# Feed-forward products by seven half-size products in place of eight (Strassen), in a two-layer trunk on one core

## The chip, the core and the metric

One core of one Trainium2 chip runs the whole program in one launch. The metric is the time of the execution on the device in microseconds (us), lower is better. The engines are named as the profile names them: PE (TensorE, the matmuls), PEld (its weight loads), DVE (VectorE), ACT (ScalarE), POOL (GpSimd), SP (SyncE, which issues the loads).

## The reference, cut to what matters

A trunk of two layers over 512 tokens of width 1024, all in float32. Each layer is a mixer (attention of two kinds) and then a feed-forward of inner width 2816; the change is about the feed-forward.

```python
D_MODEL, SEQ, DEPTH = 1024, 512, 2
D_FF = 2816
def swiglu(h, w1, w3, w2):
    return (jax.nn.silu(h @ w1) * (h @ w3)) @ w2
...
        x = x + even_mixer(...) if layer % 2 == 0 else x + odd_mixer(...)
        h = rms_norm(x, norm_ffn_g[layer])
        x = x + swiglu(h, ffn_w1[layer], ffn_w3[layer], ffn_w2[layer])
```

## The kernel before

Tokens stand along the free side (512 columns), features on the 128 partitions. The residual stream is eight tiles `xs[c]` of 128x512. To get float32 accuracy out of PE's one-pass float32r matmuls, each operand is split into a high and a low part, and each product is three matmuls: high by high, high by low, low by high (`prods`, L204 to L206).

A weight piece is a block of 128 output features by 1024 inputs (128x1024 in SBUF). SP loads it into one of three `raw` buffers, ACT copies it to the high part (`wh`, L176), DVE subtracts to get the low part (`wl`, L187); the parts rotate through three pairs of buffers (`wsp`).

`ffn` goes through 22 pieces `f` of the inner width. For each it makes the two projections (w1 and w3, eight k-blocks by three matmuls of 128x512 each) into two PSUM banks; then DVE multiplies by the norm's factor `rb` (L308), ACT takes Silu, POOL multiplies by `rb` (L311), DVE multiplies the two projections (L312), ACT and DVE split the product into `gh` and `gl` (L318). Then, for eight output blocks `n`, the down projection w2 sums over 22 blocks, and DVE adds the result to `xs[n]`. `Norm` makes the split input of the next stage (ACT `hh` L253, DVE `hl` L254, and a sum of squares on POOL, L265).

Each engine runs its own queue in order. The order in the queues is made by a scheduler from the order of the code; the orders of the two mixers (`EVEN_ORDER`, `ODD_ORDER`) are tables written out by hand, and the change leaves both as they are.

Of the kernel before, what the change touches and what calls it, by code (L numbers as in the profile page):

```python
# [8 lines left out]
F32 = mybir.dt.float32  # L9
# [7 lines left out]
P = 128  # L17
# [7 lines left out]
# which engines split the weights of a part in two, where not (act, dve)  # L25
# [25 lines left out]
# the order in which the parts are put to the scheduler  # L51
# [65 lines left out]
def tile_trunk(ctx, tc, x, gains, qk_gain, pool_scale, w_a, w_nat, pool_w, w_o0, w_qk, w_v, w_o1, w13, w2, out):  # L117
# [5 lines left out]
    wraw = ctx.enter_context(tc.tile_pool(name="wraw", bufs=WRAW))  # L123
    wsp = ctx.enter_context(tc.tile_pool(name="wsp", bufs=3))
# [4 lines left out]
    # PSUM banks by hand, the one given back first is taken first  # L129
# [78 lines left out]
    class Bank:  # L208
        """A PSUM bank that several sums share: its first product opens it, the others follow that one."""
# [22 lines left out]
    def half(ps, w, acts, i):  # L232
        """The first or the second half of a sum over eight."""
        prods(ps, [(wcol(w, k), acts[k]) for k in range(4 * i, 4 * i + 4)], i == 0, i == 1)

    class Norm:
        """Holds x * gain split in two parts, and the sum of squares."""

        def __init__(self, idx):
            self.idx = idx  # L240
            self.h = [None] * KC
            self.acc = None

# [4 lines left out]
        def scaled(self, c):  # L248
            xt = xs[c]
            g = gain_t[:, self.idx, c : c + 1]  # L250
            hi = res.tile([P, T], F32R, name=f"hh{self.idx}_{c}", tag=f"hh{c}")
            lo = res.tile([P, T], F32R, name=f"hl{self.idx}_{c}", tag=f"hl{c}")
# [40 lines left out]
    def ffn(layer, nrm, nxt):  # L293
        with tc.tile_pool(name=f"ffn{layer}", bufs=1) as fp:
            gs = []
            for f in range(NF):
                wa = weights(w13[layer, f, 0], f"ffn_w1_{layer}_{f}")
                wb = weights(w13[layer, f, 1], f"ffn_w3_{layer}_{f}")
                p1 = take()
                dense(p1, wa, nrm.h)  # L300
                if f == 0:
                    nrm.stats()
                p3 = take()
                dense(p3, wb, nrm.h)
                if f == 0:
                    nrm.bcast()
                a = fp.tile([P, T], F32, name=f"a_{layer}_{f}", tag="fa", bufs=2)
                ve.tensor_mul(a, p1, nrm.rb)  # L308
                s = fp.tile([P, T], F32, name=f"s_{layer}_{f}", tag="fs", bufs=2)
                ac.activation(s, a, AF.Silu)  # L310
                gp.tensor_mul(s, s, nrm.rb)  # L311
                ve.tensor_mul(a, p3, s)  # L312
                give(p1)
                give(p3)
                gh = fp.tile([P, T], F32R, name=f"gh_{layer}_{f}")
                gl = fp.tile([P, T], F32R, name=f"gl_{layer}_{f}")
                ac.copy(gh, a)
                ve.tensor_sub(gl, a, f32(gh))  # L318
                gs.append((gh, gl))
            for n in range(KC):  # L320
                ps = take((n,))
                pairs = []
                for k0 in range(0, NF, 8):
                    k1 = min(k0 + 8, NF)
                    raw = wraw.tile([P, D], F32, name=f"raw_w2_{layer}_{n}_{k0}", tag="raw")
                    cols = (k1 - k0) * P
                    nc.sync.dma_start(raw[:, :cols], w2[layer, n, :, k0 * P : k1 * P])
                    w = split(raw, f"ffn_w2_{layer}_{n}_{k0}", cols)
                    pairs += [(wcol(w, k - k0), gs[k]) for k in range(k0, k1)]
                prods(ps, pairs)  # L330
                ve.tensor_add(xs[n], xs[n], ps)  # L331
                give(ps)
                if nxt is not None:
                    nxt.chunk(n)
                else:
                    nc.sync.dma_start(out[n * P : (n + 1) * P, :], xs[n])

    def even(nrm, nxt, w_first):
        with ExitStack() as es:
            ap = es.enter_context(tc.tile_pool(name="ev", bufs=1))  # L340
            wk = es.enter_context(tc.tile_pool(name="evw", bufs=2))
            OWN = [slice(0, 64), slice(64, 128)]

            one = ap.tile([P, 1], F32, name="one")
# [7 lines left out]
            # low parts of the keys, zero on the half that is not the group's  # L352
# [3 lines left out]
            # v by group, zero on the other group's columns  # L356
# [12 lines left out]
            def both(dst, src, j):  # L369
                """Both parts of a head's half of src, the low one on the other half of the partitions."""  # L370
# [6 lines left out]
            # index queries, raw; a positive factor of a row leaves its order alone  # L377
# [10 lines left out]
            # index keys, on both halves, and the index weights  # L388
# [37 lines left out]
            # index scores; the first block keeps every causal key  # L426
# [21 lines left out]
            # each query takes its 128 first keys, eight at a time; of equal ones the first stands first  # L448
# [9 lines left out]
            # v, k with tokens on partitions  # L458
# [30 lines left out]
            # normalized keys, transposed; the gains of q and k go with them  # L489
# [22 lines left out]
            # queries  # L512
# [18 lines left out]
            def step_r(c):  # L531
                # scales of the logits' rows
# [16 lines left out]
            oh = ap.tile([P, 4, T], F32R, name="oh")  # L549
            ol = ap.tile([P, 4, T], F32R, name="ol")  # L550
# [24 lines left out]
            # the four heads of a group side by side  # L575
# [22 lines left out]
            # windowed means  # L598
            def step_u(g, i):
# [50 lines left out]
            def step_oa(n):  # L650
                if n % 2 == 0:
                    S["oa", n // 2] = weights(w_o0[4 + n // 2], f"oa_{n // 2}")
# [7 lines left out]
            for name, *args in EVEN_ORDER:  # L660
                steps["step_" + name](*args)

    def odd(nrm, nxt):
        with ExitStack() as es:
            ap = es.enter_context(tc.tile_pool(name="od", bufs=1))
            wk = es.enter_context(tc.tile_pool(name="odw", bufs=2))
# [9 lines left out]
            # -1 where the row is at or after the column; and -1 everywhere  # L676
# [12 lines left out]
            # v with tokens on partitions; four token blocks share each piece of the weight  # L689
# [33 lines left out]
            # per head: both parts of q on the two halves of the partitions, and k to match  # L723
# [36 lines left out]
            oh = [ap.tile([P, T], F32R, name=f"o1h{c}") for c in range(KC)]  # L760
            ol = [ap.tile([P, T], F32R, name=f"o1l{c}") for c in range(KC)]

            # where the key blocks of a head stand: (tile, first column)
# [5 lines left out]
            def before(t, nm):  # L769
                """Zero where the key is not before the query."""  # L770
# [16 lines left out]
            # scores of a tile  # L787
            def step_z(c, nm):
# [4 lines left out]
                for j in range(2):  # L793
                    # tile C holds both heads in a bank
# [6 lines left out]
            # softplus of them, zero where the key is not before the query  # L801
# [14 lines left out]
            # less the inclusive sums over later keys; then the weights and the values  # L816
# [49 lines left out]
            def step_x(h, n):  # L866
                if n % 2 == 0:
                    S["x", h, n // 2] = weights(w_o1[4 * h + n // 2], f"o1_{h}_{n // 2}")
# [8 lines left out]
            for name, *args in ODD_ORDER:  # L877
                steps["step_" + name](*args)

    # residual stream, [d, t]  # L880
# [87 lines left out]
```

## Time and profile before

| what | before |
|---|---|
| time, median of 3 runs (lowest to highest) | 1202.83 us (1202.49 to 1204.36) |
| span of the profiled execution | 1202.7 us |
| time of the profiled execution outside its span, by the median of the runs | 0.1 us |
| PE busy | 1177.3 us, 98% |
| DVE, ACT, POOL busy | 621.2, 481.0, 294.2 us |
| first feed-forward: projections, down | about 202 to 444, 444 to 565 us |
| second feed-forward: projections, down | about 839 to 1080, 1080 to 1203 us |

A matmul's duration in the trace covers its passage through the array, and matmuls overlap; the pace of PE is read from the distance of their starts, not from their durations.

### The profile page before, as it was taken

The page shows a single profiled execution, that of the slowest core. Times are in us where ns is not written, and L with a number is a line of the kernel's source. Part 1 is how long each engine was busy: PE and PEld are TensorE (multiplying, and loading weights), DVE is VectorE, ACT ScalarE, POOL GpSimd, SP SyncE. Part 2 cuts the span into 40 slices and gives each one's busy share as a digit, 9 for nine tenths or more (in the row PEclk, how much of TensorE's full clock was granted, in tenths as well). Part 3 has the DMA queues.
Part 4 walks back from the last instruction along what each step waited for, and adds up shares of the span by engine and source line. Part 5 has one row for each costly group of instructions (what it writes and reads, how often), then busy time and mean ns, then how long its engine had stood idle before and what let it go on. Part 6 is the DMA issues. An engine that isn't in the chain of part 4 may idle for free. (4 is left out here: it accounts for less than half of the span.)

```text
span 1202.7 us, 13889 instructions
## 1 busy us (share of the span) xinstructions
PE 1177.3 (98%) x5415; PEld 967.4 (80%) x5416; DVE 621.2 (52%) x851; ACT 481.0 (40%) x704; POOL 294.2 (24%) x324
## 2 busy tenths in 40 slices
PE   6999999999999999999999999999999999999998
PEld 3886758888888888888888888888888888888887
DVE  7499956434443433333457878867444434432221
ACT  4354564322223222223248778865323232321110
POOL 5246644111111110001023445433211111110000
PEclk8999999999999999999999999999999999999999
DMA  5222102232323223333221111112323233333330
GB/s 186 83 70 75 40 32 70 88 105 90 104 90 103 91 93 97 97 96 105 88 88 53 53 36 53 54 53 70 105 90 103 90 103 95 99 96 114 112 112 22
DMA packets 30737, 102.36 MB, mean 85 GB/s; under 512 B 3792, under 2 KB 4304, under 8 KB 30672
## 3 DMA queue, kind: packets, MB, share of 16 engines
q1 hardware_dynamic: 30240, 101.46, 26.4%
q8 instruction: 42, 0.69, 0.2%
q14 instruction: 23, 0.19, 0.1%
q10 hardware_dynamic: 432, 0.02, 0.0%
HBM read 99.37 MB, written 2.10 MB: 84 GB/s over the span
## 5 line engine op out<-in xcount | busy, mean ns | idle before, releaser
L205 PE MATMUL psum<-hl,wh_ffn_w 128*128 128x512 f32 x704 | 274.0, 389 | 0.3 <-DVE hl L254 0.3
L206 PE MATMUL psum<-hh,wl_ffn_w 128*128 128x512 f32 x704 | 274.1, 389 | 0.0
L204 PE MATMUL psum<-hh,wh_ffn_w 128*128 128x512 f32 x704 | 273.7, 389 | 0.0
L176 ACT ACTIVATE wh_ffn_w<-raw_ffn_w 128x1024 fp32r<-128x1024 f32 x88 | 93.4, 1061 | 305.4 <-PE psum L205 305.4
L311 POOL TENSOR_TENSOR s<-s,rb 128x512 f32<-128x512 f32 x44 | 76.8, 1748 | 378.3 <-ACT s L310 378.3
L205 PEld LDWEIGHTS psum<-hl,wh_ffn_w 128*128 128x128 f32 x704 | 132.2, 188 | 28.3 <-DVE hl L254 0.7
L206 PEld LDWEIGHTS psum<-hh,wl_ffn_w 128*128 128x128 f32 x704 | 132.2, 188 | 27.5
L204 PEld LDWEIGHTS psum<-hh,wh_ffn_w 128*128 128x128 f32 x704 | 132.2, 188 | 27.0
L204 PE MATMUL psum<-gh,wh_ffn_w 128*128 128x512 f32 x352 | 138.7, 394 | 0.0
L206 PE MATMUL psum<-gh,wl_ffn_w 128*128 128x512 f32 x352 | 138.0, 392 | 0.0
L205 PE MATMUL psum<-gl,wh_ffn_w 128*128 128x512 f32 x352 | 136.6, 388 | 0.0
L187 DVE TENSOR_TENSOR wl_ffn_w<-raw_ffn_w,wh_ffn_w 128x1024 fp32r<-128x1024 f32 x88 | 109.2, 1240 | 23.2 <-ACT wh_ffn_w L176 22.8
L176 ACT ACTIVATE wh_ffn_w<-raw_w 128x1024 fp32r<-128x1024 f32 (+1 forms) x48 | 47.5, 990 | 183.3 <-PE psum L205 158.5
L187 DVE TENSOR_TENSOR wl_ffn_w<-raw_w,wh_ffn_w 128x1024 fp32r<-128x1024 f32 (+1 forms) x48 | 54.6, 1137 | 122.4 <-ACT wh_ffn_w L176 122.4
L312 DVE TENSOR_TENSOR a<-psum,s 128x512 f32<-128x512 f32 x44 | 30.4, 691 | 138.2 <-PE psum L206 134.7
L308 DVE TENSOR_TENSOR a<-psum,rb 128x512 f32<-128x512 f32 x44 | 30.4, 692 | 107.4 <-PE psum L206 107.3
L206 PEld LDWEIGHTS psum<-gh,wl_ffn_w 128*128 128x128 f32 x352 | 66.1, 188 | 15.5
L205 PEld LDWEIGHTS psum<-gl,wh_ffn_w 128*128 128x128 f32 x352 | 66.1, 188 | 14.8
L204 PEld LDWEIGHTS psum<-gh,wh_ffn_w 128*128 128x128 f32 x352 | 66.2, 188 | 13.2
L265 POOL TENSOR_TENSOR acc<-acc,sq 128x512 f32<-128x512 f32 x28 | 42.0, 1501 | 140.4 <-ACT sq L264 139.7
L254 DVE SCALAR_TENSOR_TENSOR hl<-x,gain_t,hh 128x512 fp32r<-128x512 f32 x32 | 42.0, 1329 | 4.0 <-ACT hh L253 4.0
L204 PE MATMUL psum<-hh,wh_q 128*128 128x512 f32 x96 | 39.0, 406 | 1.8 <-DVE wh_q L178 1.8
(293 smaller groups left out, 2083.2 us busy)
## 6 DMA issues: line engine op xcount, KB each, us to landing
raw_ffn_w<-in_w_dram SPq DMA_DIRECT2D x88, 512.0 KB, 3.5
raw_w<-in_w_dram SPq DMA_DIRECT2D x32, 512.0 KB, 3.5
raw_w<-in_w_dram SPq DMA_DIRECT2D x16, 384.0 KB, 3.1
raw_v<-in_w_v_dram SPq DMA_DIRECT2D x8, 512.0 KB, 3.6
raw_q<-in_w_qk_dram SPq DMA_DIRECT2D x8, 512.0 KB, 3.5
raw_k<-in_w_qk_dram SPq DMA_DIRECT2D x8, 512.0 KB, 3.5
raw_o<-in_w_o_dram SPq DMA_DIRECT2D x8, 512.0 KB, 3.5
x<-in_x_dram SPq DMA_DIRECT2D x8, 256.0 KB, 5.3
```

Source lines behind the costliest of these rows:

```text
L176: ac.activation(dst, src, AF.Copy, scale=scale)
L187: (ve if lo_eng == "dve" else gp).tensor_sub(lo[:, :cols], raw[:, :cols], f32(hi[:, :cols]))
L204: te.matmul(ps, wh, ah, start=(first and i == 0), stop=False)
L205: te.matmul(ps, wh, al, start=False, stop=False)
L206: te.matmul(ps, wl, ah, start=False, stop=(last and i == n - 1))
L254: ve.scalar_tensor_tensor(lo, xt, g, f32(hi), op0=ALU.mult, op1=ALU.subtract)
L265: gp.tensor_add(self.acc, self.acc, sq)
L308: ve.tensor_mul(a, p1, nrm.rb)
L311: gp.tensor_mul(s, s, nrm.rb)
L312: ve.tensor_mul(a, p3, s)
```

## The change

The feed-forward's products are made by Strassen's scheme in Winograd's form. Two neighbouring output blocks, two neighbouring input blocks and the two halves of the tokens make a 2x2 by 2x2 product of blocks; it takes seven products of half the tokens (256 columns) in place of eight. A `Job` is such a unit: for the projections w1 and w3 it is a pair of output blocks over four pairs of inputs (`n` is 4; 11 pairs `f`, so 22 of these jobs a layer), for w2 a pair of output blocks over a group of two or three pairs (`groups`; 16 jobs a layer, four with `n` 2 and twelve with `n` 3; what they give is added to `xs` group by group).

Each job loads two pieces, forms four sums of weight blocks (`z[0]` on DVE, `z[1]` to `z[3]` on POOL), and splits seven blocks into high and low: `a` (two blocks straight from the load), `s` and `t` (the four sums), and `b` (one block). The moving side needs such sums too: `PairNorm` makes them once a layer from the norm's output, and `value` makes them for each product of the gates. The seven results stand in three PSUM banks, some pass through SBUF (`u`, on ACT), and DVE adds them together. `PLAIN` is the order of one job's products x1 to x7 with the last two, y4 and y3, of the job before; `FIRST` and `LAST` are that order at the two ends of the feed-forward.

The weight buffers get a fourth place (`fr`), and the pools of weights and of the mixers' output stay open through all stages; the feed-forward's first two jobs are put to the scheduler in the mixer's last steps.

```diff
-    def ffn(layer, nrm, nxt):
-        with tc.tile_pool(name=f"ffn{layer}", bufs=1) as fp:
-            gs = []
-            for f in range(NF):
-                wa = weights(w13[layer, f, 0], f"ffn_w1_{layer}_{f}")
-                wb = weights(w13[layer, f, 1], f"ffn_w3_{layer}_{f}")
-                p1 = take()
-                dense(p1, wa, nrm.h)
...
+    def token_sums(full, eng):
+        s = lambda i: full[:, i, :]
+        eng.tensor_sub(s(4), s(0), s(1))
+        eng.tensor_sub(s(5), s(2), s(4))
+        gp.tensor_sub(s(6), s(2), s(0))
+        eng.tensor_sub(s(7), s(3), s(5))
+    def token_split(full, hi, lo, a=1, b=8):
+        ac.copy(hi[:, a - 1 : b - 1, :], full[:, a:b, :])
+        ve.tensor_sub(lo[:, a - 1 : b - 1, :], full[:, a:b, :], f32(hi[:, a - 1 : b - 1, :]))
...
+        def two(self, name):
+            self.nsplit += 1
+            return [(self.fr if self.nsplit % 4 == 1 else wsp).tile([P, D], F32R, name=f"w{x}_{name}", tag=f"w{x}") for x in "hl"]
...
+                    def two(tag, src):
+                        h, l = stage.two(f"{tag}_{name}")
+                        ac.copy(h[:, :w], src)
+                        ve.tensor_sub(l[:, :w], src, f32(h[:, :w]))
+                        return h, l
...
+                    ve.tensor_add(z[0], a21, a22)
+                    gp.tensor_sub(z[1], z[0], a11)
+                    gp.tensor_sub(z[2], a11, a21)
+                    gp.tensor_sub(z[3], a12, z[1])
+                    wa = two("a", raw[0][:, :w])
+                    w12 = two("s", s12[:, :w])
+                    w34 = two("t", s34[:, :w])
+                    h = fr.tile([P, n, P], F32R, name=f"wh_b_{name}", tag="wbh")
+                    l = fr.tile([P, n, P], F32R, name=f"wl_b_{name}", tag="wbl")
+                    ac.copy(h, a22)
+                    ve.tensor_sub(l, a22, f32(h))
...
+                BANK = {1: "A", 6: "A", 7: "A", 4: "A", 2: "B", 5: "C", 3: "C"}
+                RHS = {1: B11, 2: B21, 3: B22, 4: T4, 5: T1, 6: T2, 7: T3}
...
+                        te.matmul(ps, wh, ah, start=first, stop=False, skip_group_check=True)
+                        te.matmul(ps, wh, al, start=False, stop=False, skip_group_check=True)
+                        te.matmul(ps, wl, ah, start=False, stop=last, skip_group_check=True)
...
+                    ve.tensor_mul(c1[:, ERL], c1[:, ERL], rb(ERL))
+                    ve.tensor_mul(c1[:, LAT], job.open[b][:, :HT], rb(LAT))
+                    ac.activation(c1, c1, AF.Silu)
+                    gp.tensor_mul(c1, c1, nrm.rb)
                 else:
+                    job.add(c0[:, ERL], a, b)
+                    ve.tensor_mul(c0, c0, nrm.rb)
+                    ac.activation(c0, c0, AF.Silu)
+                    gp.tensor_mul(c0, c0, nrm.rb)
...
+                    ve.tensor_mul(g[:, 2, :], g[:, 2, :], s1[:, ERL])
+                    ve.tensor_mul(g[:, 3, :], job.open[b][:, :HT], s1[:, LAT])
+                    ve.tensor_mul(g[:, 1, :], g[:, 1, :], gates[job.f][0][:, LAT])
+                    gs[job.f] = g_slot(job.f)
+                    token_split(g, *gs[job.f], 1, 4)
+                else:
+                    job.add(g[:, 0, :], a, b)
+                    ve.tensor_mul(g[:, 0, :], g[:, 0, :], gates[job.f][0][:, ERL])
+                    token_sums(g, ve if job.f == NF // 2 - 1 else gp)
+                    token_split(g, *gs[job.f], 4, 8)
...
+                eng = ve if job.last else gp
+                if what == 11:
+                    job.add(x0[:, LAT], x0[:, LAT], b)
+                elif what == 22:
+                    job.add(x1[:, ERL], x1[:, ERL], b)
+                    eng.tensor_add(x1[:, ERL], x1[:, ERL], a)
+                    eng.tensor_add(x0, x0, job.out["u"])
...
+            groups = [(0, 3), (3, 6), (6, 8), (8, 11)]
...
+            PLAIN = "x1 x2 y4 x6 y3 x5 x7"
+            FIRST = "x1:012 x2:012 x5:012 z1:012 z2:012 z5:012 x1:3 x2:3 x5:3 x6 z1:3 z2:3 x7 stats z6 bcast z5:3 x4 z7 x3"
+            LAST = (
+                "y4 x1:01 x2:01 y3 next z1:01 z2:01 x1:2 x2:2 z1:2 z2:2 x5:01 z5:01 x6 x5:2 x7 z6 z5:2 x4 z7 x3"
+            )
```

**POOL in the projections.** In each period of one piece `f`, POOL before had one instruction, the multiplication of Silu's result `s` by the norm's factor `rb`:

```order
L311 TENSOR_TENSOR s_2_2179<-s_2_2179,rb_2035 128x512
L311 TENSOR_TENSOR s_3_2249<-s_3_2249,rb_2035 128x512
L311 TENSOR_TENSOR s_4_2319<-s_4_2319,rb_2035 128x512
L311 TENSOR_TENSOR s_5_2389<-s_5_2389,rb_2035 128x512
L311 TENSOR_TENSOR s_6_2459<-s_6_2459,rb_2035 128x512
```

Now its queue in the first layer's projections reads as follows (line numbers here are those of the changed kernel; `s_w` is a job's sums of weights, `g_w` the sums of a gated product, `c_w` a gate; the two numbers after `w` are the layer and the pair `f`):

```order
L313 TENSOR_TENSOR g_w_0_1_2425<-g_w_0_1_2425 128x256
L315 TENSOR_TENSOR g_w_0_1_2425<-g_w_0_1_2425 128x256
L314 TENSOR_TENSOR g_w_0_1_2425<-g_w_0_1_2425 128x256
L422 TENSOR_TENSOR s_w_0_3_2763<-s_w_0_3_2763,raw_w_0_3_0_2759 128x512
L316 TENSOR_TENSOR g_w_0_1_2425<-g_w_0_1_2425 128x256
L423 TENSOR_TENSOR s_w_0_3_2764<-raw_w_0_3_0_2759,raw_w_0_3_1_2761 128x512
L424 TENSOR_TENSOR s_w_0_3_2764<-raw_w_0_3_0_2759,s_w_0_3_2763 128x512
L507 TENSOR_TENSOR c_w_0_2_2552<-c_w_0_2_2552,rb_2187 128x512
L423 TENSOR_TENSOR s_w_0_4_2898<-raw_w_0_4_0_2893,raw_w_0_4_1_2895 128x512
L422 TENSOR_TENSOR s_w_0_4_2897<-s_w_0_4_2897,raw_w_0_4_0_2893 128x512
L512 TENSOR_TENSOR c_w_0_2_2551<-c_w_0_2_2551,rb_2187 128x512
L424 TENSOR_TENSOR s_w_0_4_2898<-raw_w_0_4_0_2893,s_w_0_4_2897 128x512
```

What moved: for a pair of pieces POOL had two multiplications by `rb`; it now has these twelve instructions, the same two multiplications (L507, L512), six sums of weights and four sums of a gated product. All have both inputs in SBUF.

**DVE in the projections.** Before, one period of `f` on DVE was two splits of weights (L187), three passes over the projections' results, of which two read PSUM, and one split of the product:

```order
L308 TENSOR_TENSOR a_5_2387<-psum,rb_2035 128x512
L187 TENSOR_TENSOR wl_ffn_w_0_6_2406<-raw_ffn_w_0_6_2403,wh_ffn_w_0_6_2405 128x1024
L312 TENSOR_TENSOR a_5_2387<-psum,s_5_2389 128x512
L187 TENSOR_TENSOR wl_ffn_w_0_7_2470<-raw_ffn_w_0_7_2467,wh_ffn_w_0_7_2469 128x1024
L318 TENSOR_TENSOR gl_5_2394<-a_5_2387,gh_5_2393 128x512
L308 TENSOR_TENSOR a_6_2457<-psum,rb_2035 128x512
```

Now, in the same place of the program (`wl_s`, `wl_t` and `wl_b` are low parts of sums and of a block of weights; L320 the low parts of a gated product; L465 the additions that put results together from PSUM; L421 is `z[0]`):

```order
L532 TENSOR_TENSOR g_w_0_0_2145<-g_w_0_0_2145,c_w_0_0_2118 128x256
L412 TENSOR_TENSOR wl_s_w_0_1_2388<-s_w_0_1_2377,wh_s_w_0_1_2387 128x1024
L320 TENSOR_TENSOR gl_0_2310<-g_w_0_0_2145,gh_0_2309 128x768
L421 TENSOR_TENSOR s_w_0_2_2503<-raw_w_0_2_1_2501 128x512
L412 TENSOR_TENSOR wl_t_w_0_1_2392<-s_w_0_1_2378,wh_t_w_0_1_2391 128x1024
L465 TENSOR_TENSOR c_w_0_1_2292<-u_w_0_1_2370,psum 128x256
L320 TENSOR_TENSOR gl_0_2310<-g_w_0_0_2145,gh_0_2309 128x1024
L504 TENSOR_TENSOR c_w_0_1_2292<-c_w_0_1_2292,rb_2187 128x256
L412 TENSOR_TENSOR wl_s_w_0_2_2514<-s_w_0_2_2503,wh_s_w_0_2_2513 128x1024
L465 TENSOR_TENSOR g_w_0_1_2425<-u_w_0_1_2411,psum 128x256
L505 TENSOR_TENSOR c_w_0_1_2292<-psum,rb_2187 128x256
L431 TENSOR_TENSOR wl_b_w_0_1_2396<-raw_w_0_1_1_2375,wh_b_w_0_1_2395 128x512
```

What moved: the splits of sums stand between small additions from PSUM; `wl_s` and `wl_t` are low parts of what POOL's rows above make.

## Rows read from the trace of the kernel before

**Rows 1.** the page, busy time of each engine, its share of the span, instructions

```profile
PE 1177.3 (98%) x5415; PEld 967.4 (80%) x5416; DVE 621.2 (52%) x851; ACT 481.0 (40%) x704; POOL 294.2 (24%) x324
```

**Rows 2.** busy time by stretch (start:end): length, each engine (instructions), clock, DMA

```profile
core 0: us, PE busy (x) PEld busy (x) DVE busy (x) ACT busy (x) POOL busy (x), PEclk, DMA share, GB/s
...
202.00:444.00 242.00, 242.00 (x1077) 200.56 (x1076) 102.02 (x115) 73.43 (x92) 42.71 (x26) 1.00 0.30 98
...
444.00:565.00 121.00, 121.00 (x530) 99.29 (x529) 37.73 (x40) 33.27 (x40) 8.01 (x6) 1.00 0.32 94
...
839.00:1080.00 241.00, 240.74 (x1070) 199.30 (x1069) 103.25 (x118) 73.89 (x93) 42.53 (x25) 1.00 0.30 96
...
1080.00:1203.00 123.00, 118.88 (x520) 97.20 (x518) 29.42 (x30) 20.80 (x21) 0.00 (x0) 1.00 0.30 91
```

**Rows 3.** groups of instructions on PE: count, then busy, mean ns, idle before

```profile
L204 PE MATMUL psum<-hh,wh_ffn_w 128*128 128x512 f32 x704 | 273.7, 389 | 0.0
...
L204 PE MATMUL psum<-gh,wh_ffn_w 128*128 128x512 f32 x352 | 138.7, 394 | 0.0
```

**Rows 4.** PE in order of time, first projection: start, duration (us), engine, line

```profile
300.05 0.39 PE L205 MATMUL psum<-hl,wh_ffn_w 128*128 128x512 f32 x1
...
302.77 0.39 PE L205 MATMUL psum<-hl,wh_ffn_w 128*128 128x512 f32 x1
```

**Rows 5.** PE in order of time, 256 columns in the first mixer

```profile
44.84 0.28 PE L473 MATMUL psum<-wh_nat,hl 128*128 128x256 f32 x1
...
49.52 0.28 PE L473 MATMUL psum<-wh_nat,hl 128*128 128x256 f32 x1
```

**Rows 6.** POOL in order of time, four stretches; xN merges N instructions

```profile
9.38 8.56 POOL L265 TENSOR_TENSOR acc<-acc,sq 128x512 f32<-128x512 f32 x5 [0.53 <-ACT sq L264]
...
17.91 2.80 POOL L187 TENSOR_TENSOR wl_ki<-raw_ki,wh_ki 128x1024 fp32r<-128x1024 f32 x1
...
20.67 1.72 POOL L265 TENSOR_TENSOR acc<-acc,sq 128x512 f32<-128x512 f32 x1
...
71.53 2.16 POOL L617 TENSOR_TENSOR s<-s 128x512 f32<-128x512 f32 x2
...
81.06 2.58 POOL L187 TENSOR_TENSOR wl_u<-raw_u,wh_u 128x1024 fp32r<-128x1024 f32 x1
...
224.00 2.54 POOL L311 TENSOR_TENSOR s<-s,rb 128x512 f32<-128x512 f32 x2 [10.08 <-ACT s L310]
...
298.80 1.79 POOL L311 TENSOR_TENSOR s<-s,rb 128x512 f32<-128x512 f32 x1 [9.09 <-ACT s L310]
```

**Rows 7.** DVE in order of time, the same stretches and one more

```profile
9.93 8.56 DVE L254 SCALAR_TENSOR_TENSOR hl<-x,gain_t,hh 128x512 fp32r<-128x512 f32 x5
...
18.42 2.84 DVE L178 CAST wh_q<-raw_q 128x1024 fp32r<-128x1024 f32 x1
...
21.18 1.76 DVE L254 SCALAR_TENSOR_TENSOR hl<-x,gain_t,hh 128x512 fp32r<-128x512 f32 x1
...
82.07 0.69 DVE L372 TENSOR_TENSOR q<-psum,q 64x512 fp32r<-64x512 f32 x1
...
298.22 1.23 DVE L187 TENSOR_TENSOR wl_ffn_w<-raw_ffn_w,wh_ffn_w 128x1024 fp32r<-128x1024 f32 x1 [0.23 <-ACT wh_ffn_w L176]
...
622.42 1.65 DVE L720 SCALAR_TENSOR_TENSOR vz<-psum,rcol,vz 128x256 fp32r<-128x256 f32 x4
```

**Rows 8.** groups of instructions on DVE in the feed-forward

```profile
L187 DVE TENSOR_TENSOR wl_ffn_w<-raw_ffn_w,wh_ffn_w 128x1024 fp32r<-128x1024 f32 x88 | 109.2, 1240 | 23.2 <-ACT wh_ffn_w L176 22.8 <-issue 0.2
...
L318 DVE TENSOR_TENSOR gl<-a,gh 128x512 fp32r<-128x512 f32 x44 | 30.1, 685 | 1.4 <-ACT gh L317 1.4
...
L187 DVE TENSOR_TENSOR wl_ffn_w<-raw_w,wh_ffn_w 128x768 fp32r<-128x768 f32 x16 | 15.3, 958 | 0.0
```

**Rows 9.** groups of instructions on ACT in the feed-forward

```profile
L176 ACT ACTIVATE wh_ffn_w<-raw_ffn_w 128x1024 fp32r<-128x1024 f32 x88 | 93.4, 1061 | 305.4 <-PE psum L205 305.4
```

**Rows 10.** waits of PE: who for whom, us in total, times, longest

```profile
PE psum L205 <- DVE hl L254: 5.2, 7, 1.6
```

More of the change, by code (lines that the diff above doesn't have):

```diff
@@ L338, in even @@
[L338 to L341, printed above, removed]
+    B11, B22, B21, T1, T2, T3, T4 = range(7)
+    HT = T // 2
+    ERL, LAT = slice(0, HT), slice(HT, T)
+    def token_sums(full, eng):
[4 more added lines that the diff above has]
+        eng.tensor_sub(s(7), s(3), s(5))
@@ new lines, in token_split, with open, chunk @@
+    def token_split(full, hi, lo, a=1, b=8):
+        ac.copy(hi[:, a - 1 : b - 1, :], full[:, a:b, :])
+        ve.tensor_sub(lo[:, a - 1 : b - 1, :], full[:, a:b, :], f32(hi[:, a - 1 : b - 1, :]))
+    class PairNorm(Norm):
+        def open(self):
+            super().open()
+            self.es_t = ExitStack()
+            self.tpool = self.es_t.enter_context(
+                tc.tile_pool(name=f"hb{self.idx}", bufs=2, side="right", reuse_waits="tile")
+            )
+            self.pairs = []
+        def chunk(self, c):
+            self.squared(c)
+            if c % 2 == 0:
+                self.full = self.tpool.tile([P, 8, HT], F32, name=f"hb{self.idx}_{c}", tag="hb")
+            g = gain_t[:, self.idx, c : c + 1]
+            dst = self.full[:, 2 * (c % 2) : 2 * (c % 2) + 2, :].rearrange("p a b -> p (a b)")
+            ac.activation(dst, xs[c], AF.Copy, scale=g)
+            if c % 2 == 0:
+                return
+            i = c // 2
+            hi = self.pool.tile([P, 7, HT], F32R, name=f"hp{self.idx}_{i}", tag=f"hp{i}")
+            lo = self.pool.tile([P, 7, HT], F32R, name=f"hq{self.idx}_{i}", tag=f"hq{i}")
+            token_sums(self.full, ve)
+            token_split(self.full, hi, lo)
+            self.pairs.append((hi, lo))
+            if c == KC - 1:
+                self.es_t.close()
@@ new lines, in tile_trunk, with __init__, open_more, open @@
+    class Ffn:
+        def __init__(self, layer, nrm, nxt):
+            self.layer, self.nrm, self.nxt = layer, nrm, nxt
+            self.es = ExitStack()
+        def open_more(self):
+            self.pool = lambda name, bufs: self.es.enter_context(
+                tc.tile_pool(name=f"{name}{self.layer}", bufs=bufs, reuse_waits="tile")
+            )
+            self.more = self.pool("fm", 1)
+        def open(self):
+            self.nraw, self.nsplit = 0, 0
+            self.fr = self.pool("fr", 1)
+            self.fs = self.pool("fs", 1)
+            self.steps = ffn(self)
+        def first(self):
+            next(self.steps)
+        def run(self):
+            for _ in self.steps:
+                pass
+            self.es.close()
+        def raw(self, name):
+            self.nraw += 1
+            return (self.fr if self.nraw % 4 == 1 else rawp).tile([P, D], F32, name=name, tag="raw")
+        def two(self, name):
+            self.nsplit += 1
+            return [(self.fr if self.nsplit % 4 == 1 else wsp).tile([P, D], F32R, name=f"w{x}_{name}", tag=f"w{x}") for x in "hl"]
@@ L650, in step_oa @@
             def step_oa(n):
-                if n % 2 == 0:
-                    S["oa", n // 2] = weights(w_o0[4 + n // 2], f"oa_{n // 2}")
+                for i in {0: (0,), 2: (1,), 4: (2, 3)}.get(n, ()):
+                    S["oa", i] = weights(w_o0[4 + i], f"oa_{i}")
+                if n in (4, 6):
+                    after.first()
                 ps = take(EVEN_BANKS["oa"])
@@ L758, in step_k @@
                     S["k", c, j] = t
-            oh = [ap.tile([P, T], F32R, name=f"o1h{c}") for c in range(KC)]
-            ol = [ap.tile([P, T], F32R, name=f"o1l{c}") for c in range(KC)]
+            o1 = [[p.tile([P, 4, T], F32R, name=f"o1{x}{i}", tag=f"o{x}") for i, p in enumerate((big, after.more))] for x in "hl"]
+            oh, ol = [[o[c // 4][:, c % 4, :] for c in range(KC)] for o in o1]
             PLACE = {0: ("A", 0), 1: ("B", 0), 2: ("C", 0), 3: ("B", 384)}
@@ L866, in step_x @@
             def step_x(h, n):
-                if n % 2 == 0:
-                    S["x", h, n // 2] = weights(w_o1[4 * h + n // 2], f"o1_{h}_{n // 2}")
+                for i in {0: (0,), 2: (1,), 4: (2, 3) if h else (2,), 6: () if h else (3,)}.get(n, ()):
+                    S["x", h, i] = weights(w_o1[4 * h + i], f"o1_{h}_{i}")
+                if h and n in (4, 6):
+                    after.first()
                 ps = take(ODD_BANKS["x"] if h == 0 else (ODD_BANKS["y"][n],))
```

272 lines of the change are left out of this document (216 added, 56 removed).

## The prediction

> **What bounds the kernel now.** I read the page's busy times first: PE is busy 98% of the span, DVE about half, POOL a quarter [rows 1]. Next the stretches. In both feed-forwards PE is never idle and its clock is at 1.00, the 2.4 GHz level, while DVE is busy for 102 of 242 us and POOL for 43 of 242 [rows 2]. DMA is at a third. So in 726 of the 1203 us the pace of PE is the time, and nothing else counts. That pace is the distance of starts: twelve matmuls of 512 columns lie between 300.05 and 302.77, 0.2267 us each [rows 4]. A layer has 1056 of them in its projections (704 in each of L204 to L206 for two layers) and 528 in its down products [rows 3], so 1584 x 0.2267 = 359.1 us a layer. Those stretches are what the change rewrites; the reader should see that DVE and POOL had room there, and ask how much of it the change takes.
>
> **PE's part.** The new products have 256 columns. Before has such matmuls with a new weight each time: 39 starts from 44.84 to 49.52, 0.120 us each [rows 5]. A job has 7 products of n blocks by 3 matmuls. Projections: 22 x 7 x 4 x 3 = 1848; down: 7 x 3 x 44 (n summed over 16 jobs) = 924. 2772 x 0.120 = 332.6 us a layer, 26.5 less than now. It is less than an eighth, because 0.120 is more than half of 0.2267. The Trainium skill ("TensorE: Matmul & The Clock Gate", Back-to-back issue gap) gives N/2.4 + 2.5 ns for a warm matmul; by it 512 columns are 215.8 ns, 256 are 109.2, and the term would be 341.8 - 302.7 = 39.1 us a layer. The rows, where each matmul brings its own weight, show 11 ns more in both, so the sum goes by the rows.
>
> **DVE's and POOL's part: who keeps whom out.** The change puts far more on both. What matters is whether they can work at once. When POOL's 512-column sum runs with DVE idle it takes 1.27 us (two in 2.54); later, started at 298.80 under a DVE weight split that ends at 299.45, it takes 1.79 [rows 6, 7]. At the start of the kernel, five POOL sums and five DVE passes `hl`, all 512 columns from SBUF, take 8.56 us on either engine, shifted by half a microsecond: 1.71 us for a pair, though DVE's pass is 0.69 us of work in its other rows [rows 6 to 8]. The DVE cast at 18.42 ends at 21.26, right after POOL's 1024-column instruction ends at 20.71; POOL's next, started at 20.67, ends at 22.39; DVE's next ends at 22.94. They alternate. So I take: a POOL instruction with two SBUF inputs and a DVE one with two SBUF inputs exclude each other for the whole instruction. A DVE pass that reads PSUM is not held: the one at 82.07 takes its 0.69 us in the middle of POOL's 81.06 to 83.64 [rows 6, 7]. The Trainium skill ("SBUF — State Buffer", SBUF: two separate sides) says that the shared pair of ports is an exclusive lock for a whole instruction; by that rule the full sum below is a floor, and the trace agrees.
>
> Holds from these rows: POOL 512 columns 22.39 - 21.26 = 1.13 us, 1024 columns 20.71 - 18.49 = 2.22 (18.49 is the end of the five passes), so 0.59 for 256 and 0.86 for 384. DVE 512 columns 22.94 - 22.39 = 0.55; the splits of 512, 768 and 1024 take 0.685, 0.958 and 1.240 [rows 8], so 0.82 for 768, 1.10 for 1024, 0.41 for 384, 0.28 for 256.
>
> Per pair f (a w1 job and a w3 job): POOL has six z sums and two gate products of 512 and four token sums of 256, 8 x 1.13 + 4 x 0.59 = 11.4 us. DVE has six splits of 1024 (6.6), two z[0] and two `b` splits (2.2), two gate passes (0.28 + 0.55), three products of 256 (0.84), and the gated product's splits of 768 and 1024 (1.92): 12.4 us. Together 23.8 us, against PE's 20.2 (168 x 0.120) and the 21.8 (96 x 0.2267) of now. Eleven pairs: 261.5 us.
>
> A down job with n = 3: POOL 3 x 0.86 + 0.59 + 1.13 = 4.3, DVE 3 x 0.82 + 2 x 0.41 = 3.3, together 7.6, and PE 7.56. With n = 2: 3.5 + 2.2 = 5.7, PE 5.04. In the last group the sums into `xs` go to DVE: 6.7, PE 7.56 rules. 8 x 7.6 + 4 x 5.7 + 4 x 7.56 = 113.8 us, where the down products now take 119.7.
>
> So a layer is at least 375 us if one of the two always wants the turn: 16 more than 359.1. That is the low end, 1202.7 + 32 = 1235. The other end is that nothing of DVE's work on PSUM lies under POOL's turns: eight passes a pair at 0.41 (four in 1.65 [rows 7]) and four a down job make 434 us a layer, 1202.7 + 151 = 1354. I take three tenths of the way, 393: most PSUM passes will lie under a POOL turn, but both queues are in order, a low part waits for ACT's copy (1.06 us, [rows 9]) and that for POOL's sum, and four weight places for three splits a job leave little to work ahead on; in such gaps no one has the turn. 393 - 359 = 34 a layer, 68 in all.
>
> **The rest.** ACT has per pair six copies of 1.06, two of about half, six of 256 columns, two Silus and two splits, some 13 of 24 us: room. DMA moves the same bytes. At the feed-forward's start the last `PairNorm` pair needs sums, a copy and a split of 1792 columns, some 5 us more than `hl` now; 54 matmuls over the first three pairs (6.5 us) cover it if the turn is free. PE already waits there for `hl`, 5.2 us over seven times [rows 10]; I add 2 a layer, between 0 and 5. The mixers keep their orders: 0. The weights loaded early at the end of a mixer replace loads that PE did not wait for: 0; if their splits crowd `PairNorm`, they are in the 5.
>
> **Sum.** 1202.7 + 68 + 4 = 1275 us. The profiled execution is 0.1 from the median of the runs, so no correction. The runs spread by 0.16%; 0.2% is about what tells a change from none.
>
> **Rivals.** (1) Exclusion is weaker than I read it, and PE sets the pace: 1202.7 - 2 x 26.5 = 1150. For it: POOL's two sums at 71.53 take 1.08 each under DVE passes with one SBUF input [rows 6], so the hold could be a little shorter than 1.13. Against: with 1.08 the pair is still 23.3; to beat 21.8 the holds would have to be 8% too long and no turn ever idle. (2) PE's pace with waits for weights. A job's `a` takes the place that the `t` of the job two before left, free only after y3; then PE has x5 and x7 left, 24 x 0.120 = 2.88 us. The copy 1.06, the split 1.24 and one DVE split ahead of it make 3.54, and the low part is wanted 0.24 into x1: 0.4 us a job for 44 jobs, somewhat less for the smaller ones, 30 us in all: 1180. This one ends faster too, and decides the sign if the exclusion costs nothing. (3) The turn is never idle: 1235. (4) The two mechanisms feed each other: the `a` split waits for a POOL turn, PE waits for `a`, the place comes free later, and the sum goes toward or past the other end: 1320 to 1390.
>
> **Chances.** Forecast (1240 to 1320) 0.58; (3), 1205 to 1240, 0.12; (4) 0.12; (1) 0.07; (2) 0.09; about no change, between (2) and (3), 0.02. Faster 0.16, same 0.02, slower 0.82. The range leaves out (1), most of (2) and the far part of (4): 1195 to 1340. The likeliest case's own range is 1240 to 1320.
>
> **What would show it.** In the changed kernel's feed-forward PE should show idle time, ended by DVE `wl` and ACT `wh`; the distance of its starts within a product should be 0.120. POOL's 512-column sums should take 1.8 to 2.3 us instead of 1.27, DVE's 1024-column splits 1.2 to 2.4, and DVE and POOL together should be busy for more than the whole time of the projections. A pair f should take 24 to 27 us. If instead the sums stay near 1.3 us while splits stay at 1.24, exclusion is the wrong step; if PE is never idle, the whole bound is. If PE's waits come from ACT in the main, the places are the cause, and the size is that of rival (2).

## The result and the profile after

The changed kernel takes 1351.33 us, median of 4 runs (1345.96 to 1352.06), against 1202.66 us of before beside it: 1.1223 times as long, 95% interval 1.1202 to 1.1244. The sign of the prediction was right; the size was not: 1275 was forecast and the range ended at 1340.

The page of the profiled execution (span 1349.5 us): busy time of each engine, then PE's granted clock in 40 slices, in tenths.

```profile
PE 1189.8 (88%) x7792; PEld 1076.3 (80%) x7792; DVE 1101.2 (82%) x1443; ACT 683.5 (51%) x1108; POOL 817.1 (61%) x690
...
PEclk9999997999989989889999999997899899989989
```

Against [rows 1], PE is busy about as long for 2377 more, shorter instructions; DVE has gone from 621 to 1101 us and POOL from 294 to 817. The clock, 1.00 throughout the feed-forwards before [rows 2], dips in both.

Busy time by stretch, the changed kernel: first feed-forward, second mixer, second feed-forward.

```profile
198.00:644.00 446.00, 378.68 (x2829) 362.44 (x2828) 383.16 (x449) 206.65 (x334) 304.65 (x210) 0.94 0.25 78
644.00:906.00 262.00, 257.40 (x1322) 219.51 (x1321) 193.34 (x218) 176.83 (x237) 103.90 (x120) 1.00 0.20 66
906.00:1349.50 443.50, 370.71 (x2791) 356.55 (x2790) 370.86 (x442) 197.81 (x318) 300.62 (x205) 0.93 0.25 77
```

The same three stretches of the kernel before.

```profile
202.50:565.00 362.50, 362.50 (x1603) 299.45 (x1602) 139.25 (x155) 106.70 (x132) 50.22 (x32) 1.00 0.31 97
565.00:831.00 266.00, 260.85 (x1340) 224.30 (x1339) 188.76 (x212) 175.28 (x234) 93.77 (x112) 0.99 0.19 62
831.00:1202.70 371.70, 367.62 (x1623) 303.06 (x1621) 140.66 (x154) 99.11 (x121) 48.35 (x29) 1.00 0.30 95
```

So 83.5 and 71.8 us came in the two feed-forwards, and each mixer became some 4 us shorter: 146.8 together, the difference of the spans. In the first feed-forward PE stands for 67 of 446 us, and DVE's and POOL's busy times add up to 688 us, far above the stretch.

PE's waits in the changed kernel, the largest (us in total, times, longest).

```profile
PE psum L459 <- DVE wl_a_w L412: 35.4, 29, 2.9
PE psum L459 <- DVE wl_s_w L412: 18.7, 20, 2.7
PE psum L457 <- ACT wh_s_w L411: 16.4, 13, 2.7
PE psum L457 <- ACT gh L319: 10.2, 7, 4.0
PE psum L457 <- ACT u_w L477: 9.7, 5, 3.3
```

They are for parts of weights and of the gated product, and for a turn at a PSUM bank (`u`). Who made these late is seen in order of time: POOL, DVE, ACT and PE of the changed kernel around 397 us.

```profile
395.95 2.25 POOL L507 TENSOR_TENSOR c_w<-c_w,rb 128x512 f32<-128x512 f32 x1
398.17 1.17 POOL L316 TENSOR_TENSOR g_w<-g_w 128x256 f32<-128x256 f32 x1
399.30 2.25 POOL L512 TENSOR_TENSOR c_w<-c_w,rb 128x512 f32<-128x512 f32 x1
...
395.32 1.76 DVE L412 TENSOR_TENSOR wl_t_w<-s_w,wh_t_w 128x1024 fp32r<-128x1024 f32 x1
397.83 0.93 DVE L421 TENSOR_TENSOR s_w<-raw_w 128x512 f32<-128x512 f32 x1 [0.75 <-DMA raw_w<-in_w_dram]
398.68 1.74 DVE L412 TENSOR_TENSOR wl_a_w<-raw_w,wh_a_w 128x1024 fp32r<-128x1024 f32 x1
400.45 2.18 DVE L320 TENSOR_TENSOR gl<-g_w,gh 128x1024 fp32r<-128x1024 f32 x1
...
399.37 1.04 ACT L319 CAST gh<-g_w 128x1024 fp32r<-128x1024 f32 x1 [2.59 <-POOL g_w L316]
400.32 0.37 ACT L477 COPY u_w<-psum 128x256 f32<-128x256 f32 x1
...
397.23 0.28 PE L458 MATMUL psum<-hq,wh_a_w 128*128 128x256 f32 x1
400.74 0.46 PE L457 MATMUL psum<-hp,wh_b_w 128*128 128x256 f32 x1 [3.23 <-ACT u_w L477]
401.00 0.42 PE L458 MATMUL psum<-hq,wh_b_w 128*128 128x256 f32 x1
401.22 0.42 PE L459 MATMUL psum<-hp,wl_b_w 128*128 128x256 f32 x1
401.43 0.41 PE L457 MATMUL psum<-hp,wh_b_w 128*128 128x256 f32 x1
```

Read the ends: DVE 397.08, POOL 398.20, DVE 398.76, POOL 399.34, DVE 400.42, POOL 401.55, DVE 402.63. From each end to the next lie 1.12 (POOL, 512 columns), 0.56 (DVE 512), 0.58 (POOL 256), 1.08 (DVE 1024), 1.13, 1.08: the holds that the prediction took from the kernel before. Through four of these PE stands, 3.5 us from start to start. The turn reaches it by way of ACT: ACT stands 2.59 us for POOL's token sum (L316), which comes behind L507 in POOL's queue, and each of the two had a DVE instruction to wait for; then ACT copies `gh`, and only behind that, in order, makes the copy `u` (L477) that PE waits for. PE's next matmuls start 0.21 us apart, where 0.117 is usual in the projections: the granted clock is 0.54 from 400.74 to 403, near the lower level of 1.2 GHz.

### The profile page after: what moved, and what is told of

Its sections match the earlier page's. It is cut to its first block, busy times and chain, and to the rows that moved or that the text cites. A ratio compares the mean times of both kernels' runs of the same rounds, so it can differ in the third digit from the quotient of the medians.

```text
span 1349.5 us, 20416 instructions
## 1 busy us (share of the span) xinstructions
PE 1189.8 (88%) x7792; PEld 1076.3 (80%) x7792; DVE 1101.2 (82%) x1443; ACT 683.5 (51%) x1108; POOL 817.1 (61%) x690
## 5 line engine op out<-in xcount | busy, mean ns | idle before, releaser
L423 POOL TENSOR_TENSOR s_w<-raw_w,raw_w 128x512 f32<-128x512 f32 (+2 forms) x76 | 111.7, 1469 | 106.8 <-DVE wl_t_w L412 57.0
L422 POOL TENSOR_TENSOR s_w<-s_w,raw_w 128x512 f32<-128x512 f32 (+2 forms) x76 | 111.5, 1468 | 74.6 <-issue 18.2
L412 DVE TENSOR_TENSOR wl_s_w<-s_w,wh_s_w 128x1024 fp32r<-128x1024 f32 (+2 forms) x76 | 110.9, 1460 | 41.8 <-ACT wh_s_w L411 40.8
L459 PE MATMUL psum<-hp,wl_a_w 128*128 128x256 f32 x352 | 104.7, 311 | 25.1 <-DVE wl_a_w L412 25.1
L412 DVE TENSOR_TENSOR wl_a_w<-raw_w,wh_a_w 128x1024 fp32r<-128x1024 f32 (+2 forms) x76 | 119.2, 1568 | 3.1 <-ACT wh_a_w L411 2.9
L424 POOL TENSOR_TENSOR s_w<-raw_w,s_w 128x512 f32<-128x512 f32 (+2 forms) x76 | 117.4, 1545 | 1.6
L412 DVE TENSOR_TENSOR wl_t_w<-s_w,wh_t_w 128x1024 fp32r<-128x1024 f32 (+2 forms) x76 | 105.9, 1393 | 12.4 <-ACT wh_t_w L411 11.4
L457 PE MATMUL psum<-hp,wh_a_w 128*128 128x256 f32 x352 | 105.7, 309 | 9.4 <-ACT wh_a_w L411 6.1
L458 PE MATMUL psum<-hq,wh_a_w 128*128 128x256 f32 x352 | 106.5, 307 | 6.0 <-DVE hq L320 6.0
L457 PE MATMUL psum<-hp,wh_t_w 128*128 128x256 f32 x352 | 102.5, 291 | 4.8 <-DVE c_w L465 2.8
L421 DVE TENSOR_TENSOR s_w<-raw_w 128x512 f32<-128x512 f32 (+2 forms) x76 | 71.4, 940 | 27.4 <-DMA raw_w<-in_w_dram 23.3
```

The lines of the kernel that those rows point to most:

```text
L412: ve.tensor_sub(l[:, :w], src, f32(h[:, :w]))
L421: ve.tensor_add(z[0], a21, a22)
L422: gp.tensor_sub(z[1], z[0], a11)
L423: gp.tensor_sub(z[2], a11, a21)
L424: gp.tensor_sub(z[3], a12, z[1])
L457: te.matmul(ps, wh, ah, start=first, stop=False, skip_group_check=True)
```

## The experiments

Names used in what was expected: **T**, the turn that POOL's instructions and DVE's with two SBUF inputs share, with what is lost between turns, sets the time; **R**, the four weight places and their rotation set it; **C** and **Q** are told where they come. A layer's stretch below is that of the first feed-forward.

**Is it the exclusion?** Two kernels with the same waits. In the one the low part of `a`, `s` and `t` (from the third job on) is the high part less itself, from SBUF twice; in the other the high part times two PSUM banks of zeros. The low parts are zero in both, and the stage has six banks left.

```
-  ve.tensor_sub(l[:, :w], src, f32(h[:, :w]))
+  ve.tensor_sub(l[:, :w], f32(h[:, :w]), f32(h[:, :w]))
...
-  ve.tensor_sub(l[:, :w], src, f32(h[:, :w]))
+  ve.tensor_mul(l[:, :w], f32(h[:, :w]), psum[:, 6:8, :].rearrange("p a b -> p (a b)")[:, :w])
```

Expected of the first:

> Control for the next run: from the third weight split of a layer on, the low part of a, s and t is the high part less itself (so it is zero: a term is left out), still with both DVE inputs in SBUF. Theory T (turns: POOL's and DVE's instructions with two SBUF inputs exclude each other, and the turns that no one uses are lost): nothing changes, 1335 to 1365 us. Theory R (places: PE waits for weight buffers and for low parts in order, and its cold clock stretches that): nothing changes either, 1335 to 1365.

and of the second:

> As the control, with the same waits and the same lengths, but the second DVE input is an idle stretch of PSUM that holds zeros (the low part is zero again). T: the splits need no turn, a pair's turns fall from 23.8 us to 17.2, under PE's 20.2, so 1160 to 1210 us. R: the order and the waits are as before, so 1320 to 1360.

Measured, in one run each: 1365.95 and 1269.56 us; the control is 1 us above its range. The layer's stretch of the control and the low part of `a` in it:

```profile
201.00:648.00 447.00, 377.90 (x2811) 361.56 (x2810) 377.06 (x445) 204.76 (x330) 306.40 (x212) 0.94 0.25 77
...
L413 DVE TENSOR_TENSOR wl_a_w<-wh_a_w 128x1024 fp32r<-128x1024 f32 x40 | 63.6, 1590 | 3.8 <-ACT wh_a_w L411 3.8
```

and of the one that reads PSUM:

```profile
200.00:603.00 403.00, 360.29 (x2819) 348.18 (x2818) 328.89 (x452) 208.72 (x334) 257.60 (x214) 0.96 0.28 87
...
L413 DVE TENSOR_TENSOR wl_a_w<-wh_a_w,psum 128x1024 fp32r<-128x1024 f32 x40 | 48.5, 1213 | 7.1 <-ACT wh_a_w L411 7.0
```

The same pass takes 1.59 or 1.21 us by where its second input lies (the split took 1.24 in the kernel before, with POOL mostly idle [rows 8]), and 96 us of the kernel hang on it, more than R allowed. But 1269.56 is also far above T's 1160 to 1210: with most splits out of the turn a layer still takes 403 us.

**All of it on one engine.** POOL's sums, gate products and results of the feed-forward go to DVE, twelve instructions a pair in the projections and five a down job.

```
-  gp.tensor_sub(z[1], z[0], a11)
+  ve.tensor_sub(z[1], z[0], a11)
...
-  gp.tensor_mul(c1, c1, nrm.rb)
+  ve.tensor_mul(c1, c1, nrm.rb)
```

> All of POOL's sums and products of the feed-forward are moved to DVE, which was 82% busy. T: an instruction of 512 columns costs DVE 0.63 us where POOL's took 1.13 of the turn, and no turn is lost; DVE then works about 22.3 us a pair and sets the pace, 365 to 375 us a layer: 1215 to 1260. R: DVE gets more to do in front of each low part, so PE waits longer: 1350 or more.

Measured: 1239.46 us (1.0305 of before, 1.0288 to 1.0323): 112 us less, with POOL left nearly empty. That is in T's range, and R falls. The layer's stretch and a sum that was POOL's:

```profile
197.00:585.00 388.00, 359.25 (x2812) 347.05 (x2811) 373.60 (x647) 207.69 (x331) 17.43 (x12) 0.96 0.29 89
...
L424 DVE TENSOR_TENSOR s_w<-raw_w,s_w 128x512 f32<-128x512 f32 x44 | 30.3, 688 | 0.1
```

In the changed kernel that sum takes POOL this long:

```profile
L424 POOL TENSOR_TENSOR s_w<-raw_w,s_w 128x512 f32<-128x512 f32 x44 | 74.0, 1681 | 1.3
```

DVE is busy 373.6 of 388 us now: its own queue is the bound.

**No weight sums.** `s` and `t` are split straight from the second load; the four sums of a job are left out.

```
-  ve.tensor_add(z[0], a21, a22)
-  gp.tensor_sub(z[1], z[0], a11)
-  gp.tensor_sub(z[2], a11, a21)
-  gp.tensor_sub(z[3], a12, z[1])
-  w12, w34 = two("s", s12[:, :w]), two("t", s34[:, :w])
+  w12, w34 = two("s", raw[1][:, :w]), two("t", raw[1][:, :w])
```

> The four sums of weights of each job are left out and s and t are split straight from the second load (the products are then others). The splits, their places and PE's order of products stay. T: a pair's turns fall from 23.8 to 15.9 us, PE sets the pace: 1155 to 1205. R: the places are as scarce as before: 1280 to 1340.

Measured, in one run: 1182.40 us, as T had it, and R, whose places were all still there, falls a second time. By itself this run does not tell the turn from the plain wait of a split for POOL's sum, which is gone too; the pair of kernels above does. The stretch is 359 us, with PE busy for 347.

```profile
200.00:559.00 359.00, 347.06 (x2824) 341.01 (x2823) 297.18 (x411) 206.23 (x331) 131.93 (x100) 0.99 0.32 99
```

**Places, and PE's feedback.** First the places by themselves:

```
-  (self.fr if self.nsplit % 4 == 1 else wsp)
+  (self.fr if name[0] == "a" else wsp)
```

> Both parts of each job's a get a place of their own, s and t share the three others; nothing else is changed. A job's a then waits for y4's and x2's job two products earlier to leave, not for the t of the job before. Theory R (four places and their rotation make the waits): PE's waits for the low and high part of a (42 us in the changed kernel) go, 40 to 85 us: 1265 to 1310 us. Theory T (turns between POOL and DVE and their loss set the time): the turns are the same, so 1330 to 1352 us.

Measured: 1349.92 us (1.1232, 1.1216 to 1.1247), no difference to the changed kernel. Then a third of PE's work taken out:

```
-  te.matmul(ps, wh, al, start=False, stop=False, skip_group_check=True)
```

> The products of the high weight with the low token part are left out in the feed-forward, so PE has two thirds of its matmuls there (222 us a layer at 0.120); DVE and POOL have all their work. Theory T in its strict form (turns with their losses are the bound by themselves, PE only follows): 1320 to 1352 us, 430 to 446 a layer. Theory C (PE at its lower clock after each stop frees weight places late, which makes the turns idle; the loop of both is the excess over 375 us a layer): falls toward the sum of holds, 375 to 400 us a layer, 1205 to 1265 us.

Measured: 1306.67 us, 45 less, under the strict T's 1320 and far above C's 1265. So PE's own pace and its late releases cost some 22 us a layer, and the rest stays without them. The stretch:

```profile
198.00:619.00 421.00, 304.86 (x1886) 278.33 (x1886) 394.13 (x448) 208.79 (x333) 316.45 (x210) 0.84 0.27 81
```

**An account of the turn.** I put all of POOL's instructions and DVE's with two SBUF inputs of the first feed-forward in the order of their ends. An instruction holds the turn from the end of the one before, or from its own start where that is later; time between is free. In the changed kernel the turn is held 409 us and free 38. With a third of PE's work gone it is held 404 and free 17. With the sums all on DVE: held 333, free 55; with the PSUM input: held 318, free 85.

**Half a move each.** With that account two doses were forecast:

```
-  gp.tensor_sub(z[1], z[0], a11)
+  ve.tensor_sub(z[1], z[0], a11)
```

(and so z[2] and z[3]) in the one, and in the other, with the `z` sums left on POOL,

```
-  gp.tensor_mul(c1, c1, nrm.rb)
+  ve.tensor_mul(c1, c1, nrm.rb)
...
-  eng = ve if job.last else gp
+  eng = ve
```

(and so `c0` and the token sums).

> Only the three weight sums of each job move from POOL to DVE; gate products, token sums and results stay on POOL. In the changed kernel the turn is held 409 of a layer's 446 us and free for 38. POOL's weight sums hold it 112 us of that, and the same sums on DVE about 55. Theory T (the sum of holds plus some 38 us): 390 a layer, 1225 to 1255 us. Rival Q (DVE's own queue, with its passes on PSUM, is what binds, so that any work moved onto DVE costs its full 0.69 us per sum there): no gain or a loss, 1330 us or more.

> The other part: gate products, token sums and results move to DVE, the three weight sums stay on POOL. Their holds fall from about 73 to 36 us a layer, so theory T gives 410 a layer: 1265 to 1300 us. Rival Q: 1330 us or more. The two parts together gave 1239 us; if the parts do not add, DVE's own queue has become the bound in between.

Measured: 1277.96 us (1.0627, 1.0608 to 1.0645) and 1298.61 us (1.0796, 1.0778 to 1.0814). Both gain, so Q falls in its strict form, and 73 + 53 = 126 us is close to the 112 of both. The second is in T's range, the first 23 above it. The stretches, the weight sums' first:

```profile
198.00:605.00 407.00, 361.79 (x2817) 346.91 (x2817) 383.47 (x557) 203.44 (x332) 146.42 (x102) 0.97 0.27 85
```

and with the rest moved:

```profile
197.00:619.00 422.00, 370.11 (x2831) 355.08 (x2831) 397.80 (x540) 208.45 (x334) 187.87 (x122) 0.96 0.27 83
```

For the weight sums the turn is held 358 us, 6 more than forecast, and free 49, 11 more; with the rest moved it is held 379 and free 43, so that stretch too is 12 us above the 410 of its forecast. DVE is busy for 94% of the stretch in both, and in 32 of the 49 free us it runs passes that read PSUM, against 15 of 38 in the changed kernel. So, as the sum of holds shrinks, DVE's own queue seems to come up beside it; no run was made to show that this is why the first missed.

**Where seven products might pay.** Only the down products by halves, all sums on DVE, projections plain (the class `Up` makes one block of w1 or w3 by 128x512 products, as before):

```
+  class Up:
...
-  norms = [Norm(0), PairNorm(1), Norm(2), PairNorm(3)]
+  norms = [Norm(i) for i in range(4)]
```

> Projections plain as in the kernel before (512 columns), only the down products by seven products of halves, with their sums and the token sums on DVE; POOL keeps one gate product per w1 unit. PE by its own pace: 1056 x 0.2267 + 924 x 0.120 = 350.3 us a layer against 359.1: 1185 us if DVE keeps up. DVE has about 8.4 us in a down job of three blocks against PE's 7.56: 8 jobs, 7 us a layer more at most. Theory T: 1185 to 1200. Rival (the form of the seven products itself brings stops, whatever the engines): above 1203.

and only `w3` by halves, with w1 and down plain:

```
-  ups = [(up, f, w) for f in range(a, b) for w in range(2)]
+  ups = [u for f in range(a, b) for u in ((Up, 2 * f), (Up, 2 * f + 1), (w3, f))]
```

> Only the w3 projections by seven products of halves, w1 and the down products plain with 512 columns (down in four groups), all sums on DVE. PE per pair 48 x 0.2267 + 84 x 0.120 = 20.96 us, 230.6 a layer, and 119.7 for down: 350.3 against 359.1. DVE has about 15.5 us a pair, so room. Theory T: 1175 to 1195 us. Rival (the form itself brings stops): above 1203.

Measured: 1207.70 us (1.0041, 1.0026 to 1.0056) and 1207.19 (1.0039, 1.0026 to 1.0053), 8 and 12 us above T's ranges. Both lie where the rival had them, above 1203, but not by its cause: PE hardly waits in either (it is busy for 357.65 of 363 us and for 353.94 of 360 in the first layer). What is off is the distance of the 512-column matmuls. The first of these two kernels, projections:

```profile
249.75 0.39 PE L206 MATMUL psum<-hh,wl_w 128*128 128x512 f32 x1
...
252.78 0.40 PE L204 MATMUL psum<-hh,wh_w 128*128 128x512 f32 x1
```

Thirteen distances, 0.233 us each, where [rows 4] have 0.2267. The second kernel has both distances in one row of products: down, w3, w1.

```profile
316.17 0.39 PE L206 MATMUL psum<-gh,wl_w 128*128 128x512 f32 x1
...
318.89 0.39 PE L206 MATMUL psum<-gh,wl_w 128*128 128x512 f32 x1
319.12 0.28 PE L460 MATMUL psum<-hp,wh_a_w 128*128 128x256 f32 x1
...
324.60 0.28 PE L462 MATMUL psum<-hp,wl_s_w 128*128 128x256 f32 x1
324.72 0.40 PE L204 MATMUL psum<-hp,wh_w 128*128 128x512 f32 x1
...
329.85 0.40 PE L205 MATMUL psum<-hq,wh_w 128*128 128x512 f32 x1
```

With `gh` moving 12 distances give 0.2267; with `hp` 22 give 0.2332, and 47 of 256 columns 0.1166. The clock is 1.00 there. In the built programs the weights lie at 64 modulo 128 bytes of their partition, `gh` too, `hp`, `hq`, `hh` and `hl` at 96; in the kernel before, `hh`, `hl` and the weights all at 96. Hence **theory A**: the distance goes by how the two places stand to each other. It was tried both ways, each by 32 bytes: in the kernel with only the down products by halves (`mhalf`), and in the kernel before, by a buffer that nobody uses (`pad`):

```
-  mhalf = const.tile([P, 8], F32, name="mhalf")
+  mhalf = const.tile([P, 16], F32, name="mhalf")
...
+  ctx.enter_context(tc.tile_pool(name="pad", bufs=1)).tile([P, 8], F32, name="pad")
   wraw = ctx.enter_context(tc.tile_pool(name="wraw", bufs=WRAW))
```

> The kernel with plain projections and only the down products by seven products of halves, all lower buffers moved up by 32 bytes (the constant mhalf is 16 columns wide in place of 8). In its build before, the moving parts hh, hl stood at 96 modulo 128 bytes and the weights at 64, and its 512-column matmuls were 0.2335 us apart; in the kernel before both stand at 96 and the distance is 0.2267. Theory A (the distance goes by the two places): 0.2267 again, 2112 x 0.0068 = 14.4 us in the projections and some 3 in the mixers: 1185 to 1194 us, faster than the kernel before. Rival (the distance has another cause): 1204 to 1209.

> The kernel before with an unused buffer of 32 bytes ahead of the weights' buffers, nothing else: weights now at 0 modulo 128 bytes, hh and hl still at 96. Theory A: the projections' matmuls stand 0.2335 apart, 14 us more, and some 3 in the mixers: 1214 to 1222 us. Rival: 1201 to 1205.

Measured: 1194.63 us (0.9933, 0.9919 to 0.9946), faster than the kernel before; and 1217.36 us (1.0123, 1.0109 to 1.0137). Both go the way A says, by about what it says; the first is 0.6 us above the range it gave. Shifted, the projections have 14 distances in 3.17 us, 0.2264:

```profile
249.64 0.39 PE L205 MATMUL psum<-hl,wh_w 128*128 128x512 f32 x1
...
252.81 0.39 PE L204 MATMUL psum<-hh,wh_w 128*128 128x512 f32 x1
```

and the kernel before with 32 unused bytes has 16 in 3.74, 0.2337:

```profile
299.73 0.40 PE L206 MATMUL psum<-hl,wh_ffn_w 128*128 128x512 f32 x1
...
303.47 0.40 PE L207 MATMUL psum<-hh,wl_ffn_w 128*128 128x512 f32 x1
```

## Why the prediction was right in sign and wrong in size

**What bounds the kernel before**: right. **PE's part**: right within 3%; the distance is 0.117 in the changed projections and 0.120 in the down products, and PE's pace is not what bounds there. The 0.2267 of the projections was taken for the down products of the kernel before too, where the mean is 0.229; that is 1 us a layer. The Trainium skill ("TensorE: Matmul & The Clock Gate", Back-to-back issue gap) would have 109.2 and 215.8 ns for matmuls in isolation; the shortest means measured here are 0.226 us for 512 columns and 0.117 for 256.

**Who keeps whom out**: right, and shown: the holds after the change are those read before it, and a DVE pass that reads PSUM instead is not held. The Trainium skill ("SBUF — State Buffer", SBUF: two separate sides) has a lock for whole instructions; the alternation around 397 us agrees: its holds are those of the prediction to 0.02 us.

**The sum**: here it failed, in the term "I take three tenths of the way, 393", at both ends of it. The low end, 375 us "if one of the two always wants the turn", was too low: the turn is held 409 us. By the instructions in the stretch at the holds of the prediction (POOL 105 x 1.13 + 36 x 0.86 + 67 x 0.59, DVE 78 x 1.10 + 47 x 0.82 + 75 x 0.55 + 24 x 0.41 + 66 x 0.28, and 6.6 for four others) it would be 390: the passes of the norms at both ends, of which I had put only a small part into the term for the ends, take some 25 us in the same turn, while some 8 us of the first two jobs' turns lie ahead of the stretch, which is the difference to within 2 us. The other 19 are holds longer than their least, 1.17 on the mean for POOL's 512 columns instead of 1.13, 1.12 instead of 1.10 for DVE's 1024. And the turn is free 38 us a layer, not 18. With 34 more held (409 - 375) and 20 more free (38 - 18) it is 393 + 34 + 20 = 447, and 446 was measured. The upper end, 434, assumed a turn that is never free, so it was no bound.

**The rivals.** (1) and (2) fall: exclusion is as strong as read, and a place of its own for `a` changes nothing (1349.92 us). (3) falls by the account. (4) had the time, 1320 to 1390, and half of its mechanism: PE's lateness does come back to the turn, 45 us in all (without the high by low products), 21 of a layer's 38 free us; but not by the weight places, as I had put it. By which wait it comes back was not separated; the clock and the PSUM banks that `u` waits for are left. A third way shows in the traces: the loads. The first layer's stretch of the changed kernel, DVE's `z[0]` and then the queue that issues the loads (us in total, times, longest):

```profile
DVE s_w L421 <- DMA raw_w<-in_w_dram: 10.0, 10, 1.8
...
SPq L404 <- POOL s_w L424: 48.0, 20, 5.8
```

A load goes out when one of the three `raw` places is free, often only after POOL's third sum, and DVE then stands for its landing, 10.0 us in this stretch. With a third of PE's work gone none of these 10 us are left, and none with all sums on DVE. No run had more places for loads.

**The rest.** The mixers were put at no change and gained 4 us each; why, was not tried. What to see: PE's waits end at DVE's `wl` more than at ACT's `wh`, and DVE's 1024-column splits take 1.4 to 1.8 us, as foretold; POOL's 512-column sums take 1.6 to 1.9, slower than alone but in part under the 1.8 to 2.3 foretold; and a stretch of 446 us is longer than pairs of 24 to 27 us would make it.

**Still open**: why a layer takes 403 us when most splits read PSUM. The turn is free 85 us there, DVE is busy 82% and PE 89%, so no engine is full. In that stretch DVE's `z[0]` stands 19.0 us for loads to land, nearly twice as long as in the changed kernel:

```profile
DVE s_w L424 <- DMA raw_w<-in_w_dram: 19.0, 15, 2.1
```

That is a part of it; whether more places for loads would give it back was not tried.

## What to carry to other kernels

Before moving work to an engine that looks free, add up DVE's two-SBUF-input time and POOL's as if they were one engine, every pass in the stretch counted, those at its ends too, and leave room for turns that nobody takes (38 us on 409 held here, 43 on 379 and 49 on 358 in the two halves of the move); if that passes the bound of now, put the work on the engine that holds the turn for less (0.55 against 1.13 us here), not on the idle one. A saving in matmuls pays only where the other engines have room: down products alone by halves, sums on DVE, end at 0.9933 of before once the buffers lie as they did there (1.0041 where they do not), all products by halves at 1.12. When a buffer is added or shrunk, look at the distance of matmuls again before blaming the change.

## What the runs showed of the hardware that was not expected

In these kernels the distance of back-to-back float32r matmuls goes by where the moving part and the weights lie to each other in SBUF: both at the same place modulo 128 bytes, 0.2267 us for 512 columns and 0.120 for 256; 32 bytes apart, 0.2335 and 0.117. `oh` of the first mixer went the same way without being meant to: 32 bytes from its weights before (0.2335), at the same place in the changed kernel (0.2272). At 64 bytes apart, `gh` and `gl` of the kernel before have 0.229 for 512 columns. In the kernel before 32 unused bytes cost 15 us of 1202. Only these three offsets were seen, so which part of the address counts is open.
